# State space table products two groups behind their preparation, with three buffers, and the scan tables in the same room

## The chip, the cores and the metric

One core of one Trainium2 chip runs the whole step. The metric is the device time of one execution in microseconds (us); a repeated run of the unchanged kernel differs by 0.1%. The engines are PE (matrix products), DVE (VectorE), ACT (ScalarE), POOL (GpSimd) and SP, which here only issues transfers. Each executes its own queue strictly in order, so an instruction that waits holds up all that stand behind it on its engine.

## The reference, cut to what matters

A two-layer backbone for 256 context tokens and 2048 latent tokens of width 1024. In each layer the normalised, modulated input h goes through one wide projection; its columns feed four parallel branches (differential attention, a bidirectional diagonal state space model called S5, a gated linear recurrence, latent attention), and an output projection adds the result to the residual. The change concerns only tables that S5 derives from its weights, before any token is looked at:

```
step = exp(log_dt);  mag = exp(a_re * step)
ab   = mag * (cos(a_im * step) + i sin(a_im * step))        # per state, 16 groups x 64 states x 2 directions
f    = (ab - 1) / a;     bb = f * b                         # 16 channels per group
h[t] = ab * h[t-1] + bb u[t];     y = Re(c h) + d * u       # both directions
```

The kernel computes S5 in blocks of eight tokens. For this it needs, per group, the products of powers of ab with bb (wz) and with c (so, cp), the local 8-token kernel (psk, which becomes mp, with d on its diagonal), and per state the unit phases of 256 blocks (E). They go to DRAM as SC and ED, and the scan reads them some 1.6 ms later.

## The kernel before

`build` (L1696) runs three stages per layer: `first_stage`, `mixers`, `out_proj`. Only `first_stage` (L1607) is changed. It weaves two generators, with weights 49 and 250: `proj1` (L420) and `s5_build` (L1160).

`proj1` walks the 2304 tokens in six blocks of 384. For a block it transposes and modulates the input (`h_block`, tile pst, L299), keeps it in DRAM (HD, L440), makes five 128-wide products in the transposed layout (psF, L177 to L179, each float32 product as three of split operands), each with rotary embedding on DVE and stores to KD and QD on SP's queue (L355), and three products in token layout (psT), whose results are stored to VT (L500). These stores go on SP's queue, in the last block on POOL's.

`s5_build` first computes the powers on DVE in small operations. Then `prep(gi)` (L1270) prepares the operands of a group: wz with six and so with five operations on POOL and one on DVE (L1286), cp with six on DVE (L252 to L257), and two copies brep. The scratch tile tw has a single buffer and is used by wz, so and cp of a group in turn. `emit(gi)` (L1296) forms the products: two transposes of wz (pswz, L1302), copied by ACT into so (L1303), which SP stores to SC (L1304); four passes for psk (L1307), copied by ACT into mp (L1308). mp has one buffer for four groups: after every fourth group DVE adds Db (L1311) and SP issues eight stores (L1313). In the program emit(gi - 1) follows prep(gi). wz, so, cp and brep come from the pool sb1 with two buffers.

Then POOL doubles a base table of 16 phases (b_, with t3 as scratch, L1325), and for each pair of groups copies it into two tiles Eb (L1332) and doubles them four times up to 256 phases (L1333); SP stores them to ED (L1336). Eb0 and Eb1 have one buffer each.

What sets the order: the program's order is a priority only. A scheduler simulates the timeline of all engines and puts into each engine's queue what is ready there, the earliest in the program first (L23), so POOL's queue today mixes Eb's operations with those of prep. PE's queue alone is written by hand in the second projection. The room: sb1 and then sb are the first pools of the right side, and when the stage ends the second projection (`proj2`, L506) puts its pools there, first the tiles h of 18 KB per partition (loads at L521). A new tile waits for the old tiles whose room it takes.

Of the kernel before, what the change touches and what calls it, by code (L numbers as in the profile page):

```python
# [10 lines left out]
F32 = mybir.dt.float32  # L11
# [92 lines left out]
def run(g):  # L104
    for _ in g:
        pass


PR = (0, 0)
AVB = 2  # L110
PPB = 3
DA_A = 740
# [40 lines left out]
def pool(g, name, bufs, side="left"):  # L153
    return g.tc.tile_pool(name=name, bufs=bufs, side=side, reuse_waits="tile")
# [611 lines left out]
def diff_attn(g, l, p, p1):  # L766
# [74 lines left out]
    def pass2(pr, qb):  # L841
# [11 lines left out]
        def av_mm(batch):  # L853
            first = None
            for ki, aa, _ in batch:
                kt = kts[ki]
                for hh in range(2):
                    x = nc.tensor.matmul(av[hh * 64:(hh + 1) * 64, :n], lhsT=v[:, kt, hh * 64:(hh + 1) * 64], rhs=aa[:, hh, :n], start=(ki == 0), stop=(ki == len(kts) - 1))  # L858
                    first = first or x
            hold(g, first, batch[-1][2])  # L860

        for ki, kt in enumerate(kts):
# [11 lines left out]
            late.append((ki, aa, last))  # L874
            if len(late) > AVB:
                av_mm(late[:AVB])
                del late[:AVB]
        g.kfree = max(g.kfree, 3 * pr + 3) if qb == QLAST else g.kfree
# [9 lines left out]
def mla(g, l, p):  # L888
# [47 lines left out]
    def pass2(pr, qb):  # L936
# [17 lines left out]
        for ki, kt in enumerate(kts):  # L954
# [18 lines left out]
            late.append((ki, e, last))  # L973
            if len(late) > AVB:
                av_mm(late[:AVB])
                del late[:AVB]
        g.kfree = max(g.kfree, 3 * (pr + 2) + 3) if qb == QLAST else g.kfree
# [182 lines left out]
def s5_build(g, l, p1, pb):  # L1160
# [6 lines left out]
    def t16(nm):  # L1167
        return pb.tile([128, 16], F32, name=nm)
# [7 lines left out]
    x, mag, th = t16("x"), t16("mag"), t16("th")  # L1176
# [3 lines left out]
    k, t = t16("k"), t16("t")  # L1180
# [42 lines left out]
        renorm(nx[0], nx[1])  # L1223
        cur = nx
    yield 5
    t3 = pb.tile([128, 16, 16], F32, name="t3")
    den, fr, fi, am1 = t16("den"), t16("fr"), t16("fi"), t16("am1")
    ab = (P[0][:, 1, :], P[1][:, 1, :])
    V.tensor_tensor(den, are, are, ALU.mult)
# [24 lines left out]
    for i in range(2):  # L1254
# [5 lines left out]
        V.memset(pt[i], 0.0)  # L1260
        V.tensor_copy(pt[i][0:64, :, 7:15], pv[0:64, :, 0:8])
        V.tensor_copy(pt[i][64:128, :, 0:8][:, :, ::-1], pv[64:128, :, 0:8])
    Db = pb.tile([128, 16, 16], F32, name="Db")
    nc.sync.dma_start(Db.rearrange("p g h -> p (g h)"), g.A["s5_d"][l:l + 1, :].to_broadcast([128, 256]))
    V.tensor_tensor(Db, Db, g.id16.unsqueeze(1).to_broadcast([128, 16, 16]), ALU.mult)
    SC = g.SC[l]
# [3 lines left out]
    def prep(gi):  # L1270
        tw = pb.tile([128, 15, 16], F32, tag="tw", name="tw")
        wz = [p1.tile([128, 16, 8], F32, tag=f"wz{i}", name=f"wz{i}").rearrange("p c s -> p s c") for i in range(2)]
        pwb = [pws[i][:, gi, :].unsqueeze(2).to_broadcast([128, 8, 16]) for i in range(2)]
        bbb = [bb[i][:, gi, :].unsqueeze(1).to_broadcast([128, 8, 16]) for i in range(2)]
        cmul(E, wz[0], wz[1], pwb[0], pwb[1], bbb[0], bbb[1], tw[:, :8, :])
        so = p1.tile([128, 4, 128], F32, tag="so", name="so")
        pqb = [pq[i][:, gi, :].unsqueeze(2).to_broadcast([128, 8, 16]) for i in range(2)]
        ccb = [x_[:, gi, :].unsqueeze(1).to_broadcast([128, 8, 16]) for x_ in c_]
        car, cai = (so[:, i, :].rearrange("p (t h) -> p t h", h=16) for i in (2, 3))
        tw8 = tw[:, :8, :]  # L1280
        E.tensor_tensor(car, pqb[0], ccb[0], ALU.mult)
        E.tensor_tensor(tw8, pqb[1], ccb[1], ALU.mult)
        E.tensor_tensor(car, car, tw8, ALU.subtract)
        E.tensor_tensor(cai, pqb[0], ccb[1], ALU.mult)
        E.tensor_tensor(tw8, pqb[1], ccb[0], ALU.mult)
        V.scalar_tensor_tensor(cai, cai, -1.0, tw8, ALU.mult, ALU.subtract)  # L1286
        cp = [p1.tile([128, 15, 16], F32, tag=f"cp{i}", name=f"cp{i}") for i in range(2)]
        ptb = [pt[i][:, gi, :].unsqueeze(2).to_broadcast([128, 15, 16]) for i in range(2)]
        ccc = [c_[i][:, gi, :].unsqueeze(1).to_broadcast([128, 15, 16]) for i in range(2)]
        cmul(V if CPV else E, cp[0], cp[1], ptb[0], ptb[1], ccc[0], ccc[1], tw)  # L1290
        br_ = [p1.tile([128, 16, 8], F32, tag=f"brep{i}", name=f"brep{i}").rearrange("p c s -> p s c") for i in range(2)]
        V.tensor_copy(br_[0], bbb[0])
        V.tensor_scalar(br_[1], bbb[1], -1.0, None, ALU.mult)
        return wz, so, cp, br_

    def emit(gi, wz, so, cp, br_):  # L1296
        if gi % 4 == 0:
            g.s5mp = p1.tile([128, 4, 240], F32, tag="mp", name="mp", bufs=1)
        mp = g.s5mp
        for i in range(2):  # L1300
            ps_ = pst(g, "mm", "pswz")
            nc.tensor.transpose(ps_[:, 0:128], wz[i].rearrange("p s c -> p c s").rearrange("p c s -> p (c s)"), g.ident)  # L1302
            nc.scalar.copy(so[:, i, :], ps_[:, 0:128])  # L1303
        nc.sync.dma_start(SC[gi, :, 0:4, :], so)  # L1304
        psk = pst(g, "mm", "psk")
        for i in range(2):
            nc.tensor.matmul(psk[:, :240], lhsT=br_[i].rearrange("p s c -> p c s").rearrange("p c s -> p (c s)"), rhs=cp[i].rearrange("p t h -> p (t h)"), start=(i == 0), stop=(i == 1))  # L1307
        nc.scalar.copy(mp[:, gi % 4, :], psk[:, :240])  # L1308
        if gi % 4 == 3:
            g4 = gi - 3  # L1310
            V.tensor_tensor(mp[:, :, 112:128], mp[:, :, 112:128], Db[:, g4:g4 + 4, :], ALU.add)  # L1311
            for s in range(8):
                nc.sync.dma_start(SC[g4:g4 + 4, s:128:8, 4, :].rearrange("g p c -> p g c"), mp[s:128:8, :, (7 - s) * 16:(7 - s) * 16 + 128])  # L1313

    late = None
    for gi in range(16):
        x = prep(gi)
        yield 5
        if late:
            emit(gi - 1, *late)  # L1320
        late = x
    emit(15, *late)
    E.memset(b_[0][:, :, 0:1], 1.0)
    E.memset(b_[1][:, :, 0:1], 0.0)
    double_table(E, b_, ph, slice(0, 16), t3, 0, 4)  # L1325
    yield 5
    for g0 in range(0, 16, 2):
        gs = slice(g0, g0 + 2)
        Eb = [pb.tile([128, 2, 257], F32, tag=f"Eb{i}", name=f"Eb{i}") for i in range(2)]
        te = t3.rearrange("p (a b) c -> p a (b c)", a=2)  # L1330
        for i in range(2):
            E.tensor_copy(Eb[i][:, :, 0:16], b_[i][:, gs])  # L1332
        double_table(E, Eb, ph, gs, te, 4, 8)  # L1333
        for i in range(2):
            E.tensor_copy(Eb[i][:, :, 256], ph[8][i][:, gs])
            nc.sync.dma_start(g.ED[i, :, gs], Eb[i])  # L1336
        yield 5
# [96 lines left out]
def mixers(g, l):  # L1434
    with ExitStack() as es:
# [23 lines left out]
        with (g.tc.manual_schedule(engines={mybir.EngineType.PE}) if MAN else ExitStack()):  # L1459
            run(weave((att, 520 + 700 - DA_A), (ahead(g, ssm(), PR[1]), YW)))  # L1460

# [143 lines left out]


def first_stage(g, l):  # L1607
    with pool(g, "sb1", 2, "right") as q1, pool(g, "sb", 1, "right") as qb:
        run(weave((proj1(g, l), 49), (s5_build(g, l, q1, qb), SBW)))


# [196 lines left out]
```

## Time and profile before

| what | value |
|---|---|
| median of 3 runs | 5299.3 us (5298.6 to 5303.79) |
| profiled execution | 5296.69 us |
| its span, first to last instruction | 5294.9 us |
| PE busy | 4724.9 us (89%) |
| DVE busy | 3835.7 us (72%) |
| ACT busy | 3183.3 us (60%) |
| POOL busy | 1089.4 us (21%) |
| mean granted TensorE clock | 0.935 |

The busy shares are means over the whole span. The first stage lies at about 0 to 430 us in layer 0 and 2700 to 3080 us in layer 1; POOL is busy there for three quarters of the time, and little elsewhere. An arrow in a row of waits points to the instruction that ended the wait.

### The profile page before, as it was taken

The numbers are of one execution on the slowest core, as the hardware profiler recorded it, in microseconds if no ns is written. First come the engines' busy times: TensorE is split into PE (matmuls) and PEld (weight loads), VectorE is DVE, ScalarE is ACT, GpSimd is POOL, SyncE is SP. The second block draws the span as 40 slices with busy tenths as digits, with TensorE's granted clock in tenths as the row PEclk, the third lists the DMA queues.
The fourth block names the chain that finished last, engine by engine and source line by source line (L and its number), as shares of the span: only waits on it lengthen the run. The fifth ranks groups of instructions, "written<-read, shape, count | busy, mean of one in ns | idle before, by whom it ended". The sixth has DMA issues, their size and how long they took to land.

```text
span 5294.9 us, 81097 instructions
## 1 busy us (share of the span) xinstructions
PE 4724.9 (89%) x27920; PEld 3434.4 (65%) x27920; DVE 3835.7 (72%) x7616; ACT 3183.3 (60%) x7516; POOL 1089.4 (21%) x1323
## 2 busy tenths in 40 slices
PE   6787999999998997898987879999999989989899
PEld 5676767677665664445776757676776656654477
DVE  7655767676668886896676657676766688879877
ACT  3225878777777783235433258787777777743354
POOL 4651222222210000000227712222222100000022
PEclk8998999999998997899999989999999989989999
DMA  6555233433332124415445452334333321241253
GB/s 219 170 174 154 87 105 96 130 116 104 92 88 75 47 57 129 130 50 148 157 155 200 159 167 86 108 94 130 116 103 93 88 73 48 54 117 52 75 155 126
DMA packets 507523, 599.37 MB, mean 113 GB/s; under 512 B 147630, under 2 KB 414806, under 8 KB 507110
## 3 DMA queue, kind: packets, MB, share of 16 engines
q1 hardware_dynamic: 506630, 592.61, 37.3%
q8 instruction: 220, 3.60, 0.3%
q14 instruction: 193, 1.58, 0.1%
q0 software_dynamic: 480, 1.57, 0.1%
HBM read 378.42 MB, written 215.18 MB: 112 GB/s over the span
## 4 chain that ended last, share of the span: by engine, by line
PE 49%; DVE 18%; DMA 13%; ACT 10%; issue 4%; POOL 4%; SPq 1%; ACTq 0%; DVEq 0%; POOLq 0%
PE psav L858 5%; PE psS L870 4%; PE psF L177 4%; PE psF L178 4%; PE psF L179 4%; PE psS L817 4%; PE psmav L950 3%; ACT junk L820 3%; PE psM L961 2%; DVE nm L818 2%; DVE a L872 2%; DVE mnm L927 2%; ACT pp L871 2%; PE psM L926 2%; PE pshg L1018 2%
## 5 line engine op out<-in xcount | busy, mean ns | idle before, releaser
L818 DVE TENSOR_REDUCE nm<-psS 128x1 f32<-128x512 f32 (+1 forms) x1312 | 790.5, 626 | 351.7 <-PE psS L817 340.5
L820 ACT ACTIVATE junk<-psS,nm 128x512 bf16<-128x512 f32 (+1 forms) x1312 | 848.7, 647 | 202.2 <-DVE nm L818 182.4
L871 ACT ACTIVATE pp<-psS 128x512 f32<-128x512 f32 (+1 forms) x1184 | 654.5, 594 | 165.7 <-PE psS L870 159.6
L177 PE MATMUL psF<-h,whi 128*128 128x288 f32 x2304 | 697.9, 303 | 32.8 <-ACT whi L169 32.8
L872 DVE SCALAR_TENSOR_TENSOR a<-pp,nlam 128x512 f32<-128x512 f32 (+1 forms) x592 | 510.3, 864 | 257.6 <-ACT pp L871 256.9
L178 PE MATMUL psF<-h,whi 128*128 128x288 f32 x2304 | 687.9, 299 | 0.0
L179 PE MATMUL psF<-h,wlo 128*128 128x288 f32 x2304 | 685.1, 297 | 1.8 <-DVE wlo L173 1.8
L964 ACT ACTIVATE me<-psM 128x512 f32<-128x512 f32 (+1 forms) x592 | 345.6, 590 | 440.8 <-PE psM L963 395.1
L817 PE MATMUL psS<-ks,qs 96*128 96x512 f32 (+1 forms) x1312 | 544.5, 425 | 58.9 <-ACT junk L820 37.7
L870 PE MATMUL psS<-qs,ks 98*128 98x512 f32 (+1 forms) x1184 | 440.6, 436 | 53.9 <-ACT junk L820 38.7
L177 PEld LDWEIGHTS psF<-h,whi 128*128 128x128 f32 x2304 | 444.7, 193 | 65.3 <-ACT whi L169 34.5
L171 POOL CAST whi<-w 128x1024 fp32r<-128x1024 f32 x140 | 153.2, 1094 | 1622.0 <-PE psF L178 1299.7
L178 PEld LDWEIGHTS psF<-h,whi 128*128 128x128 f32 x2304 | 444.8, 193 | 54.8
L927 DVE TENSOR_REDUCE mnm<-psM 128x1 f32<-128x512 f32 (+1 forms) x656 | 394.1, 623 | 70.9 <-PE psM L926 69.0
L179 PEld LDWEIGHTS psF<-h,wlo 128*128 128x128 f32 x2304 | 441.5, 192 | 3.1 <-DVE wlo L173 3.1
L817 PEld LDWEIGHTS psS<-ks,qs 96*128 96x128 f32 x1312 | 255.2, 197 | 165.5 <-ACT junk L820 98.4
L870 PEld LDWEIGHTS psS<-qs,ks 98*128 98x128 f32 x1184 | 203.3, 192 | 236.3 <-ACT junk L820 136.4
L173 POOL TENSOR_TENSOR wlo<-w,whi 128x1024 fp32r<-128x1024 f32 x140 | 350.3, 2502 | 11.2
L967 DVE TENSOR_TENSOR macc<-macc,me 128x1024 f32<-128x1024 f32 x256 | 311.2, 1216 | 45.0 <-ACT me L964 44.2
L950 PE MATMUL psmav<-me,mv 128*64 128x512 f32 (+1 forms) x1184 | 318.0, 631 | 13.7 <-ACT me L964 7.9
L858 PE MATMUL psav<-a,dav 128*64 128x512 f32 (+1 forms) x1184 | 309.5, 643 | 18.2 <-DVE a L872 18.2
L961 PE MATMUL psM<-qs,ks 98*128 98x512 f32 (+1 forms) x592 | 269.8, 456 | 49.2 <-ACT me L964 21.6
(451 smaller groups left out, 10191.2 us busy)
## 6 DMA issues: line engine op xcount, KB each, us to landing
w<-wF SPq DMA_DIRECT2D x152, 512.0 KB
h<-HD SPq DMA_DIRECT2D x64, 576.0 KB
wmod<-w_mod SPq DMA_DIRECT2D x48, 512.0 KB
HD<-hhi SPq DMA_DIRECT2D x12, 1536.0 KB
HD<-hlo SPq DMA_DIRECT2D x12, 1536.0 KB
GX<-ev SPq DMA_DIRECT2D x128, 144.0 KB
gt<-GX SPq DMA_DIRECT2D x36, 512.0 KB
PF<-ev SPq DMA_DIRECT2D x96, 144.0 KB
```

The lines of the kernel that those rows point to most:

```text
L177: nc.tensor.matmul(out, lhsT=w_hi, rhs=x_hi, start=start, stop=False)
L178: nc.tensor.matmul(out, lhsT=w_hi, rhs=x_lo, start=False, stop=False)
L179: nc.tensor.matmul(out, lhsT=w_lo, rhs=x_hi, start=False, stop=stop)
L817: nc.tensor.matmul(ps[:, :kn], lhsT=qs[0:96, i, t * 128:(t + 1) * 128], rhs=key_cols(ks[i], k0, kn)[0:96], start=True, stop=True)
L818: nc.vector.tensor_reduce(nm[:, i, t, ci:ci + 1], ps[:, :kn], axis=AX.X, op=ALU.max, negate=True)
L820: nc.scalar.activation(out=junk[:, :kn], in_=ps[:, :kn], func=AF.Exp, bias=nm[:, i, t, ci:ci + 1], accum_out=sm[:, i, t, ci:ci + 1])
L858: x = nc.tensor.matmul(av[hh * 64:(hh + 1) * 64, :n], lhsT=v[:, kt, hh * 64:(hh + 1) * 64], rhs=aa[:, hh, :n], start=(ki == 0), stop=(ki = ...
L870: nc.tensor.matmul(ps[:, :n], lhsT=key_cols(ks[2 * hh + m], kt * 128, 128), rhs=qs[:, 2 * hh + m, :n], start=True, stop=True)
L871: nc.scalar.activation(out=pp[:, m, :n], in_=ps[:, :n], func=AF.Exp)
L872: last = nc.vector.scalar_tensor_tensor(aa[:, hh, :n], pp[:, 1, :n], nlam, pp[:, 0, :n], ALU.mult, ALU.add)
L927: nc.vector.tensor_reduce(nm[:, i, t, ci:ci + 1], ps[:, :kn], axis=AX.X, op=ALU.max, negate=True)
L950: x = nc.tensor.matmul(av[i * 64:(i + 1) * 64, :n], lhsT=v[:, kts[ki], i * 64:(i + 1) * 64], rhs=e[:, i, :n], start=(ki == 0), stop=(ki == ...
```

## The change

A constant S5LAG = 2 is added. The loop over groups keeps the prepared operands in a list and emits the oldest when more than two are there, with a further yield of 0.1 behind each emission; the last two are emitted behind the loop, with yields of 2. The pool sb1 has three buffers. The tile t3 (scratch of bb and, later, of the doublings) and the tile Db share one buffer under one tag; for the doublings t3 is taken anew. The tiles Eb0 and Eb1 leave the pool sb and take turns in the three buffers of so in sb1.

```diff
--- before.py
+++ after.py
@@ -107,6 +107,7 @@
 
 
 PR = (0, 0)
+S5LAG = 2
 AVB = 2
 PPB = 3
 DA_A = 740
@@ -1223,7 +1224,7 @@
         renorm(nx[0], nx[1])
         cur = nx
     yield 5
-    t3 = pb.tile([128, 16, 16], F32, name="t3")
+    t3 = pb.tile([128, 16, 16], F32, tag="t3", name="t3")
     den, fr, fi, am1 = t16("den"), t16("fr"), t16("fi"), t16("am1")
     ab = (P[0][:, 1, :], P[1][:, 1, :])
     V.tensor_tensor(den, are, are, ALU.mult)
@@ -1260,7 +1261,7 @@
         V.memset(pt[i], 0.0)
         V.tensor_copy(pt[i][0:64, :, 7:15], pv[0:64, :, 0:8])
         V.tensor_copy(pt[i][64:128, :, 0:8][:, :, ::-1], pv[64:128, :, 0:8])
-    Db = pb.tile([128, 16, 16], F32, name="Db")
+    Db = pb.tile([128, 16, 16], F32, tag="t3", name="Db")
     nc.sync.dma_start(Db.rearrange("p g h -> p (g h)"), g.A["s5_d"][l:l + 1, :].to_broadcast([128, 256]))
     V.tensor_tensor(Db, Db, g.id16.unsqueeze(1).to_broadcast([128, 16, 16]), ALU.mult)
     SC = g.SC[l]
@@ -1312,21 +1313,25 @@
             for s in range(8):
                 nc.sync.dma_start(SC[g4:g4 + 4, s:128:8, 4, :].rearrange("g p c -> p g c"), mp[s:128:8, :, (7 - s) * 16:(7 - s) * 16 + 128])
 
-    late = None
+    late = []
     for gi in range(16):
-        x = prep(gi)
+        late.append((gi, prep(gi)))
         yield 5
-        if late:
-            emit(gi - 1, *late)
-        late = x
-    emit(15, *late)
+        if len(late) > S5LAG:
+            k, x = late.pop(0)
+            emit(k, *x)
+            yield 0.1
+    for k, x in late:
+        emit(k, *x)
+        yield 2
+    t3 = pb.tile([128, 16, 16], F32, tag="t3", name="t3")
     E.memset(b_[0][:, :, 0:1], 1.0)
     E.memset(b_[1][:, :, 0:1], 0.0)
     double_table(E, b_, ph, slice(0, 16), t3, 0, 4)
     yield 5
     for g0 in range(0, 16, 2):
         gs = slice(g0, g0 + 2)
-        Eb = [pb.tile([128, 2, 257], F32, tag=f"Eb{i}", name=f"Eb{i}") for i in range(2)]
+        Eb = [p1.tile([128, 2, 257], F32, tag="so", name=f"Eb{i}") for i in range(2)]
         te = t3.rearrange("p (a b) c -> p a (b c)", a=2)
         for i in range(2):
             E.tensor_copy(Eb[i][:, :, 0:16], b_[i][:, gs])
@@ -1605,7 +1610,7 @@
 
 
 def first_stage(g, l):
-    with pool(g, "sb1", 2, "right") as q1, pool(g, "sb", 1, "right") as qb:
+    with pool(g, "sb1", S5LAG + 1, "right") as q1, pool(g, "sb", 1, "right") as qb:
         run(weave((proj1(g, l), 49), (s5_build(g, l, q1, qb), SBW)))
```

## Rows read from the trace of the kernel before

**Rows 1.** Windows view, stretch; length, busy us (count) of PE, PEld, DVE, ACT, POOL; clock; DMA
```profile
105.00:345.00 240.00, 190.61 (x925) 166.38 (x926) 152.20 (x331) 64.25 (x146) 180.47 (x398) 0.90 0.48 159
2790.00:3025.00 235.00, 193.76 (x991) 169.66 (x992) 159.64 (x349) 68.18 (x157) 188.59 (x409) 0.93 0.52 175
```

**Rows 2.** Waits of PE, layer 0, 105 to 345 us: us in total, times, longest
```profile
PE pswz L1302 <- POOL wz L257: 18.0, 6, 7.5
PE pswz L1302 <- ACT mp L1308: 11.8, 3, 6.2
PE psk L1307 <- DVE cp L254: 5.3, 2, 4.3
PE pswz L1302 <- POOL wz L254: 4.5, 5, 1.8
...
PE psk L1307 <- DVE cp L257: 2.1, 3, 0.9
PE psF L177 <- ACT x L372: 1.6, 1, 1.6
```

**Rows 3.** Waits of PE, layer 1, 2790 to 3025 us
```profile
PE psk L1307 <- DVE cp L254: 11.2, 5, 4.7
PE pswz L1302 <- POOL wz L257: 9.2, 4, 5.5
PE psk L1307 <- DVE cp L257: 5.8, 4, 4.8
PE pswz L1302 <- POOL wz L254: 5.8, 4, 2.3
PE pswz L1302 <- ACT mp L1308: 4.5, 2, 3.4
```

**Rows 4.** Timeline of POOL, layer 1: start us, us, operation, idle before
```profile
2791.71 1.43 POOL L252 TENSOR_TENSOR wz<-pws,bb 128x128 f32<-128x128 f32 x2 [0.88 <-DVE bb L254]
...
2847.51 0.40 POOL L253 TENSOR_TENSOR tw<-pws,bb 128x128 f32<-128x128 f32 x1
...
2856.28 0.40 POOL L1285 TENSOR_TENSOR tw<-pq,c 128x128 f32<-128x128 f32 x1
...
2860.52 0.65 POOL L253 TENSOR_TENSOR tw<-pws,bb 128x128 f32<-128x128 f32 x1 [0.34 <-DVE cp L257]
```

**Rows 5.** Timeline of DVE, layer 1, the same group
```profile
2856.72 0.47 DVE L1286 SCALAR_TENSOR_TENSOR so<-so,tw 128x128 f32<-128x128 f32 x1 [2.84 <-POOL tw L1285]
...
2859.63 0.81 DVE L257 TENSOR_TENSOR cp<-cp,tw 128x240 f32<-128x240 f32 x1
```

**Rows 6.** POOL by line, 2780 to 3045 us: busy us, mean ns, idle before, releasers
```profile
L254 POOL TENSOR_TENSOR Eb<-Eb,t 128x32 f32<-128x32 f32 (+3 forms) x32 | 16.5, 517 | 1.1
...
L254 POOL TENSOR_TENSOR wz<-wz,tw 128x128 f32<-128x128 f32 x16 | 10.6, 664 | 0.2
...
L1284 POOL TENSOR_TENSOR so<-pq,c 128x128 f32<-128x128 f32 x14 | 6.9, 490 | 0.0
L1332 POOL COPY Eb<-b 128x32 f32<-128x32 f32 x16 | 5.5, 342 | 20.4 <-DMA ED<-Eb 20.4
...
L257 POOL TENSOR_TENSOR b<-b,t 128x16 f32<-128x16 f32 (+3 forms) x4 | 2.5, 634 | 0.0
```

**Rows 7.** Timeline of SP's queue, layer 1
```profile
3038.99 1.00 SPq L1336 DMA_DIRECT2D ED<-Eb  x2
...
3042.09 3.07 SPq L521 DMA_DIRECT2D h<-HD  x4
```

**Rows 8.** Timeline of SP's queue, layer 0
```profile
368.28 3.90 SPq L521 DMA_DIRECT2D h<-HD  x2
```

**Rows 9.** Timeline of PE, layer 1, first matmul on h
```profile
3109.55 0.61 PE L177 MATMUL psF<-h,whi 128*128 128x288 f32 x1 [8.25 <-ACT whi L169]
```

**Rows 10.** Timeline of PE, layer 0, first matmul on h
```profile
480.77 0.61 PE L177 MATMUL psF<-h,whi 128*128 128x288 f32 x1 [8.55 <-ACT whi L169]
```

**Rows 11.** Timeline of POOL, layer 1, end of the stage
```profile
3069.49 0.61 POOL L500 DMA_DIRECT2D VT<-evT  x1 [34.61 <-ACT evT L499]
```

## The prediction

> **What bounds the kernel now.** The page gives a PE-bound kernel, but the change touches only the first stage of each layer, where the first projection (proj1) runs woven with the building of the state space (S5) tables. So I read that stage, not the whole. First the view by stretches: between the first and the last table product PE works 190.6 of 240 us in layer 0 and 193.8 of 235 us in layer 1, so it idles 49 and 41 us, and no other engine is busier [rows 1]. Then the waits of PE in these two stretches. Nearly all of the idle time stands ahead of S5's own instructions: 41.7 us in the five rows shown of layer 0 and 36.5 us in the five of layer 1, against 1.6 us ahead of proj1's matmuls [rows 2, 3]. PE executes in order, so a table transpose (pswz) whose operand isn't there holds up proj1's matmuls behind it. The waits are of three kinds: for POOL's wz 18.0 + 4.5 + 9.2 + 5.8 = 37.5 us, for DVE's cp 5.3 + 2.1 + 11.2 + 5.8 = 24.4 us, and for ACT's copy into mp, which itself waits for a buffer, 11.8 + 4.5 = 16.3 us. Sum 78.2 us.
>
> Then why the operands are late. Follow one group on POOL and DVE: its first use of tw starts at 2847.51, its last POOL use (L1285) at 2856.28, DVE carries on at 2856.72 and starts the last cp at 2859.63, and only then can POOL begin the next group's tw, at 2860.52 [rows 4, 5]. tw has one buffer, so this ring of 13.0 us is the pace of preparation; the two buffers of wz, so, cp and brep seldom are. Of the ring 2856.68 - 2847.51 = 9.2 us is POOL's. A group's preparation has eleven kinds of operation there, from L254 with 10.6 us to L1284 with 6.9 us for all 16 groups, 92.2 us together; the seven of them that stand in the ring take 3.75 us a group by their means. The rest of the 9.2 us are operations on Eb and on other groups that lie between them in POOL's queue [rows 6].
>
> **The change part by part.** (a) The lag of two. emit(k) now follows prep(k+2) in program order, where it followed prep(k+1). Order in the program is only a priority here: the queues are written in the order in which operations become ready in the scheduler's simulated time. S5 starts late (the first wz of layer 1 at 2791.71, 16 groups at 13 us to go) [rows 4], while the weave gives it about one group for each of proj1's blocks; so its products are the oldest work whenever they are ready, with either lag. I therefore give the lag itself nothing; its upper bound is all 78.2 us, its lower bound 0, since an emission that is moved down adds no instruction and can at worst be as late as its operand already is.
>
> (b) Three buffers instead of two for wz, so, cp, brep. No work is added, and no wait of PE shown is for a buffer of these [rows 2, 3]; I give it nothing (bounds 0 and 13 us, a ring once a layer). mp and tw keep their single buffer, so the 16.3 us for mp stay.
>
> (c) Eb moves into the so buffers and is thereby behind all 16 so tiles in POOL's queue; and t3, Db and the new t3 share one buffer, so the doubling of the base table (its temporary is that t3) waits for the last Db addition, behind emit(15). Today Eb's work lies among the preparation. This is the part that I expect to act. Without it POOL's part of the ring falls from 9.2 to 3.75 us, DVE's stays at 2859.63 + 0.81 - 2856.72 = 3.7 (I take 4.0) with about 1 us of handing over, so the ring falls from 13.0 to 8.7 us. PE's waits for wz and cp both hang on this ring (cp waits for DVE, and DVE for POOL's tw). Foreign work was 5.4 of 9.2 us, 59%; I take that share of the waits to go: 0.59 x (37.5 + 24.4) = 36.5 us over both layers. The bounds are 0 (all returns, as PE's order is made tighter by the same amount) and 61.9.
>
> (d) What is late next. Preparation takes 16 x 8.7 = 139 us from 2791.7, to 2931; the last emits with their Db addition take some 15 us (a ring and a copy), to 2946; then the base table, 11.5 us (six kinds of operation on b, 2.5 us the largest); then the Eb operations with 103.9 us (eight kinds, the largest 16.5 us) and their waits for the ED stores, 20.4 us now [rows 6] (bounds 0 to 40, since three buffers serve two tiles of a group). Eb ends at 2946 + 11.5 + 124 = 3081 where it ended at 3035, 46 us later. Behind it: the ED store and then, in SP's queue, the loads of h for the second projection, which are to lie in the room of these tiles; today ED goes at 3039 and h at 3042 in layer 1, h at 368 in layer 0 [rows 7, 8]. The first matmul on h starts at 3109.55 and 480.77 [rows 9, 10]. With today's distance of 3 to 7 us from Eb's end, h is issued at 3088; its four issues take 3.1 us, and with 5 us of flight, my estimate, it has landed at 3096, under a start that 18 us of gain would put at 3091: 5 us lost. In layer 0 the h loads move to 414, 66 us ahead of their use. But SP executes in order: where h is queued in front of proj1's last stores (KD, QD) and Eb is later than was planned, these stores, their buffers and proj1's last block stand. POOL has the same knot, with the stores of VT at 3069.49 behind Eb [rows 11]. For both together I take 7 us, over both layers; 0 is the lower bound and 46 us in each layer the upper. The Db load now waits for bb's cmul; its first use, behind the fourth group, is four rings later and hides it.
>
> The sum: -36.5 + 5 + 7 = -24.5 us. The profiled execution took 5296.7 us (span 5294.9), so 5272.2; the median of the runs is 2.6 us above that execution, so 5274.8 us, rounded to 5275.
>
> **One rule against it.** Operations of one shape differ on POOL: 128x128 takes 490 ns in the mean at L1284 and 664 at L254 [rows 6]. The Trainium skill (SBUF — State Buffer, "Who interferes with whom") says that a VectorE instruction with two SBUF inputs and a GpSimd instruction that reads SBUF exclude each other for a whole instruction. The rows show the spread, not its cause; taken strictly the rule does not hold here, as DVE (159.6) and POOL (188.6) are busy 348 us in 235 [rows 1], which can only be if many of their instructions run beside each other. By the rule a closer ring would buy little; the third rival below works that out from rows.
>
> **The rivals.** First, the change doesn't do what it says: PE's queue is drawn up for the faster ring, and PE is as early for each operand as before, 78.2/32 = 2.4 us a group. Then the 78.2 us stay and so does the time, 5299 give or take 10, if the tail hides. For it: the stalls are differences between planned and real time, and the plan moves with the change. Against it: waits for ED, which nobody planned so long, no longer stand ahead of wz.
>
> Second, PE loses all S5 stalls, those for mp too, as POOL runs ahead and three buffers take up the jitter: -78.2 with a tail of 12 is -66, 5233. Against it: mp is still single, and its eight stores per four groups come closer together.
>
> Third, on the other side: POOL and DVE don't speed up, and the Eb tail decides. If POOL's preparation (92.2 us) and DVE's work (159.6/235 x 139 = 94 us) can hardly run together, preparation takes 186 us, a ring of 11.6. Then the gain is a third, about -12, and Eb ends at 2791.7 + 186 + 15 + 11.5 + 124 = 3128, h lands at 3143 with ED's store, and the first matmul on h slips from 3109.55 by 34 us; the stores behind h in layer 0 take 5 more. That is +27, 5326. It decides as soon as the last ED store of layer 1 is issued after some 3095. The skill's rule above is this rival's mechanism. For it: the ED waits and the single tw buffer are unchanged; against it: the overlap in rows 1.
>
> **How the numbers follow.** Forecast 0.40 (own range 5255 to 5288), nothing gained 0.22 (5289 to 5310), all stalls gone 0.16, the tail decides 0.22. What differs from no change by less than 0.2%, 10.6 us, can't be told from it. Faster are the forecast and the second: 0.56; same 0.22; slower 0.22. The range reaches from the second rival, 5236, to near the third, 5320; half of each lies outside, 2 in 10 together. The rest of the kernel is scheduled by the same simulation, and shifted starts may reorder some of it by several us either way; that is inside these widths.
>
> **What would show it.** Right: no Eb between the tw steps on POOL, a ring near 9 us, PE's waits for wz and cp down by half or more, Eb in one block at the end, ED's last store some 46 us later in layer 1. (a) is wrong if pswz is moved past proj1's matmuls so that its waits vanish with the ring still at 13 us. (d) is wrong if SP shows long waits at the h loads or POOL holds the VT stores. The forecast is wrong if PE's S5 waits stay near 78 us, or if the second projection starts later than its stage ends by more than now.

## The result: 1% slower, and the profile after

The changed kernel takes 5349.98 us (median of 5 runs, 5342.91 to 5351.73) against 5299.06 for the kernel before (5285.18 to 5303.79): ratio 1.0101, 95% interval 1.0084 to 1.0119. The forecast of 5275 us, and its sign, were wrong. The third rival, "the tail decides" (5326 us), came nearest.

The profiled execution of the changed kernel has a span of 5349.2 us, 54 more than before. Where they arise can be read from five marks in each trace: the first product psF of proj1, its last psT, the first matmul on h of the second projection, and POOL's first and last operation on wz and on Eb.

| us from the span's start | before | after |
|---|---|---|
| layer 0: last psT | 433.1 | 438.7 |
| layer 0: first matmul on h | 464.5 | 484.3 |
| layer 1: first psF | 2704 | 2721 |
| layer 1: wz on POOL | 2792 to 3010 | 2809 to 2984 |
| layer 1: Eb on POOL | 2814 to 3034 | 3000 to 3148 |
| layer 1: last ED store issued | 3040 | 3149 |
| layer 1: last psT | 3079.2 | 3084.9 |
| layer 1: first matmul on h | 3109.5 | 3164.4 |

The stage itself, from first psF to last psT, became 11 us shorter in layer 1 (375.2 to 364.1) and 7 us longer in layer 0 (409.2 to 415.9). The gap between it and the second projection grew from 31.4 to 45.6 us in layer 0 and from 30.3 to 79.5 us in layer 1: 63 us together. That is the whole loss and more. Behind the gaps little changed: from the first matmul on h of layer 1 to the last result both kernels take 2180 us, and from that of layer 0 to the first psF of layer 1 the changed kernel takes 3 us less. Nor does the granted clock explain it: its mean is 0.88 and 0.91 of full speed in the two stages, and 0.94 and 0.95 behind the gaps, in both kernels.

What answers to [rows 1] is this, from the windows view: layer 0 in the same stretch, layer 1 from the first wz to the first Eb, and the block of Eb.

```profile
105.00:345.00 240.00, 192.60 (x940) 170.61 (x941) 131.51 (x334) 65.32 (x150) 119.76 (x263) 0.89 0.46 149
2809.00:3000.00 191.00, 162.84 (x846) 144.22 (x845) 125.59 (x315) 61.14 (x142) 105.02 (x208) 0.92 0.49 169
3000.00:3150.00 150.00, 91.66 (x385) 72.78 (x383) 45.77 (x89) 34.69 (x84) 87.90 (x225) 0.75 0.58 170
```

POOL's busy time in layer 0 fell from 180 to 120 us, as Eb left this stretch, and yet PE's rose only from 190.6 to 192.6. In the third row POOL does 88 us of Eb while PE works 92 of 150 us. PE's waits in layer 0, 105 to 345 us, beside [rows 2]:

```profile
PE pswz L1303 <- POOL wz L258: 15.3, 6, 4.1
PE pswz L1303 <- ACT so L1304: 11.2, 3, 5.5
PE pst L300 <- DVE dg L288: 9.2, 3, 4.8
PE pswz L1303 <- ACT mp L1309: 5.7, 3, 2.8
PE pst L300 <- ACT t L305: 3.3, 1, 3.3
```

The waits for cp are nearly gone in layer 0; a wait of pswz behind ACT's copies of so (3.4 us before) and waits of proj1's own transposes stand in their place. Ahead of all table products (pswz and psk) PE waited 49.2 + 41.0 us in the stretches 95 to 450 and 2780 to 3100 us before, and 35.2 + 28.0 after: 27 us less, of which the length of the two stages shows 5. Ahead of proj1's own products PE waited 19 us more in the same stretches (23.9 + 11.0 before, 39.8 + 14.6 after).

Now the tail. SP's queue in layer 1, before (the second four loads of h, which [rows 7] don't have) and after (start us, us, operation):

```profile
3096.25 2.46 SPq L521 DMA_DIRECT2D h<-HD  x4
```

```profile
3112.46 2.52 SPq L522 DMA_DIRECT2D h<-HD  x4
...
3129.56 20.04 SPq L1341 DMA_DIRECT2D ED<-Eb  x4
3151.41 2.33 SPq L522 DMA_DIRECT2D h<-HD  x4
3153.78 18.21 SPq L533 DMA_DIRECT2D w<-wF  x3
```

The last four ED issues hold the queue for 20 us, in most of which SP waits for POOL to finish Eb (16.2 us at one of them). The second four loads of h follow, and the weights w follow them. PE's waits from 3084 to 3165 us, and its first matmul on h, beside [rows 9]:

```profile
PE psF L178 <- ACT whi L170: 47.4, 1, 47.4
PE psS L818 <- DMA ks<-KD: 13.2, 1, 13.2
```

```profile
3164.43 0.61 PE L178 MATMUL psF<-h,whi 128*128 128x288 f32 x1 [47.42 <-ACT whi L170]
```

Before, the first of the two waits was 8.25 us [rows 9], and the second was this:

```profile
PE psS L817 <- DMA ks<-KD: 3.4, 1, 3.4
```

The releaser named, ACT's split of w, is only the last link. The chain that ended last goes back through w, h and ED to POOL's last Eb, and from there to an earlier ED store (start us, us, what; 3080 to 3175 us, excerpt):

```profile
3129.56 9.49 DMA ED<-Eb
...
3148.53 0.73 POOL Eb L258
3149.28 2.04 DMA ED<-Eb
3151.83 0.50 SPq L522
...
3153.78 9.54 DMA w<-wF
3163.34 1.05 ACT whi L170
```

[Rows 10] had been misread: that row isn't the first matmul on h of layer 0, which came at 464.5 us.

POOL by line from 2790 to 3160 us shows why the block is so long; beside [rows 6] (busy us, mean ns, idle time before):

```profile
L255 POOL TENSOR_TENSOR Eb<-Eb,t 128x32 f32<-128x32 f32 (+3 forms) x32 | 15.1, 471 | 2.3
...
L1282 POOL TENSOR_TENSOR so<-pq,c 128x128 f32<-128x128 f32 x13 | 10.7, 822 | 24.3 <-DMA SC<-so 24.1 <-ACT evT L500 0.2
L258 POOL TENSOR_TENSOR wz<-wz,tw 128x128 f32<-128x128 f32 x16 | 9.9, 619 | 1.2
...
L254 POOL TENSOR_TENSOR tw<-pws,bb 128x128 f32<-128x128 f32 x16 | 8.0, 497 | 32.8 <-DVE cp L258 30.9 <-DVE rsv L190 1.8
...
L1337 POOL COPY Eb<-b 128x32 f32<-128x32 f32 x16 | 4.6, 293 | 54.7 <-DMA ED<-Eb 54.7
```

The Eb operations themselves are a little quicker than before, but POOL now waits 54.7 us for ED stores to land before it may reuse a buffer (20.4 before). And the ring is not free either: POOL waits 24.1 us for the stores of so, in spite of three buffers, and 30.9 us for DVE's last use of tw. These two waits before, 2780 to 3045 us:

```profile
POOL tw L253 <- DVE cp L257: 9.9, 6, 3.2
POOL so L1281 <- DMA SC<-so: 5.6, 1, 5.6
```

### The profile page after: what moved, and what is told of

It reads as the page before. It is cut to its first block, busy times and chain, and to the rows that moved or that the text cites. A ratio compares the mean times of both kernels' runs of the same rounds, so it can differ in the third digit from the quotient of the medians.

```text
span 5349.2 us, 81141 instructions
## 1 busy us (share of the span) xinstructions
PE 4732.8 (88%) x27920; PEld 3450.5 (65%) x27920; DVE 3805.8 (71%) x7616; ACT 3177.9 (59%) x7516; POOL 1079.5 (20%) x1323
## 4 chain that ended last, share of the span: by engine, by line
PE 51%; DVE 18%; DMA 12%; ACT 10%; issue 4%; POOL 3%; SPq 2%; ACTq 0%; DVEq 0%; POOLq 0%
PE psav L859 5%; PE psS L871 4%; PE psF L178 4%; PE psF L179 4%; PE psF L180 4%; PE psS L818 4%; PE psmav L951 3%; ACT junk L821 3%; PE psM L962 2%; DVE nm L819 2%; DVE a L873 2%; ACT pp L872 2%; PE psM L927 2%; DVE mnm L928 2%; PE psop L178 2%
## 5 line engine op out<-in xcount | busy, mean ns | idle before, releaser
L927 PE MATMUL psM<-ks,qs 96*128 96x512 f32 (+1 forms) x656 | 263.7, 438 | 55.0 <-DMA ks<-KRD 26.7
```

## The experiments

Times are medians; a ratio is to the kernel before, run beside it on the same chip. The places of marks are from one profiled execution each. "Last ED" below is the issue of the last ED store of layer 1, "gap" the time from the last psT to the first matmul on h.

**Lag one, rooms shared.** The changed kernel with

```diff
-S5LAG = 2
+S5LAG = 1
```

> The changed kernel with a lag of one group, and so two buffers, the rest as changed: Eb in the room of so, one buffer for t3 and Db. Theory (the tail: all of Eb's doubling now stands behind the last product, and what follows the stage waits for it): the tail is kept, so about 5345 us, 5325 to 5365. Rival (the lag: a later emission keeps the buffers longer and delays the stage): back to about 5300 us, 5285 to 5315.

Measured: 5356.33 us, ratio 1.0112 [1.0077, 1.0147]; last ED 3172, gap 82 us. The loss needs neither the lag of two nor the third buffer. What the two together are worth isn't resolved: the interval is some 18 us wide to either side and holds the changed kernel's.

**One Eb pair doubled.** The changed kernel, in which only the first pair of Eb is built, and stored for all eight:

```diff
-        Eb = [p1.tile(...) for i in range(2)]
+        if g0 == 0:
+            Eb = [p1.tile(...) for i in range(2)]
...
-        double_table(E, Eb, ph, gs, te, 4, 8)
+        if g0 == 0:
+            double_table(E, Eb, ph, gs, te, 4, 8)
```

> The changed kernel with Eb doubled for the first pair of groups alone and stored eight times (it leaves out seven of eight doublings in each layer, so ED holds the phases of the first pair everywhere). Theory (the tail): the gap between the last projection product and the first product on h falls from 46 and 80 us to the 32 and 31 us of before or less, 5350 - 63 = 5287 us, 5265 to 5300. Rival (the lag): over 5325 us, since all products are emitted as late as in the changed kernel.

Measured: 5284.9 us, ratio 0.9978 [0.9965, 0.9992]; Eb ends at 2997, gaps 30.2 and 30.1 us as before the change. Without the tail the change gains 11 us. PE's waits ahead of table products are 36.6 + 31.2 us here, near those of the changed kernel. So this is about all that the shorter ring is worth: 0.2%, not 0.7%. SP's queue and PE in layer 1:

```profile
2999.14 14.14 SPq L1345 DMA_DIRECT2D ED<-Eb  x15
...
3086.84 3.28 SPq L522 DMA_DIRECT2D h<-HD  x4
```

```profile
3100.17 0.61 PE L178 MATMUL psF<-h,whi 128*128 128x288 f32 x1 [7.12 <-ACT whi L170]
```

**Only t3 and Db share.** The kernel before with

```diff
-    t3 = pb.tile([128, 16, 16], F32, name="t3")
+    t3 = pb.tile([128, 16, 16], F32, tag="t3", name="t3")
...
-    Db = pb.tile([128, 16, 16], F32, name="Db")
+    Db = pb.tile([128, 16, 16], F32, tag="t3", name="Db")
...
+    t3 = pb.tile([128, 16, 16], F32, tag="t3", name="t3")
     E.memset(b_[0][:, :, 0:1], 1.0)
```

> The kernel before with one thing of the change: t3, Db and the t3 of the doublings share one buffer; lag one, two buffers, Eb in its own two tiles. Theory A (this shared buffer is what puts the whole doubling behind the last addition of Db): the tail appears, Eb's first operation after the last product, 5325 to 5350 us. Theory B (the room of so does it): no effect, 5290 to 5308 us.

Measured: 5380.26 us, ratio 1.0159 [1.014, 1.0179]; Eb from 3004 to 3161, gaps 60.5 and 91.1 us. One kilobyte of shared scratch alone makes the tail, and a longer one than the whole change:

```profile
3147.96 14.08 SPq L1337 DMA_DIRECT2D ED<-Eb  x4
...
3163.90 2.23 SPq L521 DMA_DIRECT2D h<-HD  x4
```

**Only Eb in so's buffers.** The kernel before with

```diff
-        Eb = [pb.tile([128, 2, 257], F32, tag=f"Eb{i}", name=f"Eb{i}") for i in range(2)]
+        Eb = [p1.tile([128, 2, 257], F32, tag="so", name=f"Eb{i}") for i in range(2)]
```

> The kernel before with one edit: the Eb tiles are taken from the two so buffers; t3 and Db keep rooms of their own, the lag stays one. Theory (the tail decides, and either sharing alone is enough for it): Eb can't start before the last so tiles are given back, near 3000 us in layer 1, so it becomes one block of some 150 us behind the products, its last store goes out near 3150, the first matmul on h slips by 40 to 60 us in layer 1 and 10 to 30 in layer 0, and the time is 5335 to 5375 us. Rival (only the buffer shared by t3 and Db keeps Eb back; with the base table doubled early, Eb slips in between the so tiles): Eb still starts before 2900 us in layer 1, time 5290 to 5310 us.

Measured: 5328.92 us, ratio 1.006 [1.0039, 1.0081]; Eb from 2984 to 3148, gaps 39.5 and 67.2 us.

```profile
3129.75 19.86 SPq L1336 DMA_DIRECT2D ED<-Eb  x4
...
3152.02 2.41 SPq L521 DMA_DIRECT2D h<-HD  x4
```

The place is as the theory had it, the time 6 us below its range. From first psF to first matmul on h the two layers lose 55 us against the kernel before, nearly as much as with the whole change (59); the rest of the kernel took 26 us less, which no run explains. Either sharing alone puts Eb behind the products. With both and the same lag it was 5356: the two don't add up, as both make the same block.

**The block's gate.** The changed kernel with the scratch of the doublings in tw's buffer (to make room for the longer tw, the small tile den takes the tile k; the three later runs with scratch in tw's buffer have this too):

```diff
-        tw = pb.tile([128, 15, 16], F32, tag="tw", name="tw")
+        tw = pb.tile([128, 16, 16], F32, tag="tw", name="tw")[:, :15, :]
...
-    t3 = pb.tile([128, 16, 16], F32, tag="t3", name="t3")
+    t3 = pb.tile([128, 16, 16], F32, tag="tw", name="t3")
     E.memset(b_[0][:, :, 0:1], 1.0)
```

> The changed kernel with the doubling's scratch taken from the buffer of tw instead of the one that t3 and Db share, so that the base table waits for POOL's own last tw only and no longer for the last Db addition behind the last products. Theory (the gate at the Db addition is a small part of the tail; the block of about 149 us of Eb is the large one): Eb starts 10 to 16 us earlier than 3000 us in layer 1, and the time is 5333 to 5345 us. Rival (Eb waits for the so buffers in any case, whose last stores go out behind the last products): Eb starts at 3000 us as before, time 5345 to 5355 us.

Measured: 5348.83 us, ratio 1.0098 [1.0076, 1.012]. From POOL's last wz to its first Eb it is 12 us (3009 to 3021) where it was 16. Layer 1 began 22 us later than in the changed kernel; counted from its first psF, Eb starts after 278 us, and there after 279. The theory fell, and the time is the rival's: taking the gate at Db away gains nothing that can be seen. That so's buffers are what holds Eb instead is argued, not shown.

**Half of Eb on DVE.** The same kernel, with

```diff
+        Q = V if g0 % 4 else E
+        te = (tv if g0 % 4 else t3).rearrange("p (a b) c -> p a (b c)", a=2)
...
-        double_table(E, Eb, ph, gs, te, 4, 8)
+        double_table(Q, Eb, ph, gs, te, 4, 8)
```

> The kernel of the run with the scratch in tw's buffer, in which every second pair of groups has its Eb doubled on DVE with a scratch of its own, the others on POOL as before. Theory (the length of the Eb block sets the start of the second projection): POOL has half of the operations, the block falls from 149 to 80 to 100 us, the last ED store goes out at 3080 to 3100 us in layer 1, the first matmul on h comes 40 to 50 us earlier than at 3164 us, and the time is 5285 to 5310 us. Rival (three buffers and their ED stores set the pace of the block, or DVE's share of it stands in front of the splits that PE waits for): the block stays over 120 us or PE's waits for DVE grow by as much as the tail falls, time 5325 to 5350 us.

Measured: 5346.28 us, ratio 1.0092 [1.0064, 1.0119]; last ED 3129, first matmul on h 3151.3. The theory fell, the rival held (block 130 us): with half of its work gone POOL waits nearly as long for ED as before, and DVE waits too. Waits of POOL, 2990 to 3130 us, and of DVE, 2990 to 3110 us:

```profile
POOL Eb L1339 <- DMA ED<-Eb: 48.2, 5, 24.1
```

```profile
DVE Eb L1339 <- DMA ED<-Eb: 34.1, 6, 10.1
```

The pace of the block is set by the three buffers and the issue and landing of their stores more than by the operations.

**ED stored by POOL's queue.** The changed kernel with

```diff
-            nc.sync.dma_start(g.ED[i, :, gs], Eb[i])
+            nc.gpsimd.dma_start(g.ED[i, :, gs], Eb[i])
```

> The changed kernel with the 16 stores of ED in each layer issued by POOL instead of SP. Theory (SP is held: its last four ED issues stand 20 us in the queue, and the loads of h and of the weights for the second projection stand behind them): the loads go out 20 to 30 us earlier, the first matmul on h of layer 1 comes at 3115 to 3140 instead of 3164 us, and the time is 5305 to 5330 us. Rival (room: the second four loads of h are to lie in the buffers that Eb holds, so they wait for the last ED store to land, whoever issues it): they still go out at about 3150 us, the first matmul on h stays within 10 us of 3164, time 5340 to 5355 us.

Measured: 5322.17 us, ratio 1.005 [1.0034, 1.0065]; last ED 3127, first matmul on h 3141.5. The time fits the theory, the mechanism is the rival's. First POOL's wait for ED, 2780 to 3180 us, then SP's wait at the loads of h, 3060 to 3190 us:

```profile
POOL Eb L1337 <- DMA ED<-Eb: 25.3, 9, 5.0
```

```profile
SPq L522 <- DMA ED<-Eb: 18.5, 2, 16.9
```

```profile
3099.30 2.25 SPq L522 DMA_DIRECT2D h<-HD  x4
3129.95 2.45 SPq L522 DMA_DIRECT2D h<-HD  x4
```

SP is no longer held by ED's issues, and still the second four loads of h wait until the last ED store has landed, because they are to lie in Eb's room. In layer 1 the block is 17 us shorter (131.5 for 148.5), as POOL waited 25 instead of 55 us for its buffers to come free, and the first matmul on h comes 16 us sooner after the first psF; in layer 0 it is 2 us. The rest of the 28 us isn't seen in the profiled execution, which was the slowest of its seven (5332.68).

**Both remedies at once.** The kernel with half of Eb on DVE, with the store of the run before it:

```diff
-            nc.sync.dma_start(g.ED[i, :, gs], Eb[i])
+            nc.gpsimd.dma_start(g.ED[i, :, gs], Eb[i])
```

> The kernel of the run with half of the Eb pairs on DVE, with ED stored by POOL's queue as well. Each of the two alone brought the last ED store of layer 1 from 3149 to 3127 to 3129 us. Theory (the start of the second projection follows the landing of the last ED store, as its buffers are the room of h): the block shrinks again, the last ED store goes out at 3100 to 3115 us, the first matmul on h of layer 1 comes at 3115 to 3135 us, time 5300 to 5325 us. Rival (with the block shorter, the order of the second projection's loads in SP's queue holds it): the first matmul on h stays at 3140 us or later, time 5325 to 5350 us.

Measured: 5316.36 us, ratio 1.0033 [1.002, 1.0047]; last ED 3112, h at 3119.86, first matmul 3133.0. The theory held.

**Half of the pairs left out.** The changed kernel, in which only every second pair of Eb is built, and stored for two:

```diff
-        Eb = [p1.tile(...) for i in range(2)]
+        if g0 % 4 == 0:
+            Eb = [p1.tile(...) for i in range(2)]
...
-        double_table(E, Eb, ph, gs, te, 4, 8)
+        if g0 % 4 == 0:
+            double_table(E, Eb, ph, gs, te, 4, 8)
```

> The changed kernel with the doubling of four of the eight pairs of Eb left out in each layer; every pair that is doubled is stored for two pairs, so all 16 stores remain. It stands between the changed kernel (eight pairs, 5350 us) and the run with one pair (5285 us). Theory (the tail costs nothing until the last ED store of layer 1 goes out after some 3095 us, and then one for one): the block ends near 3075 us, the first matmul on h comes at 3100 to 3110 us, time 5280 to 5300 us. Rival (POOL's work behind the products costs in proportion, by a busy port or a busy queue): half of the 65 us between the two kernels remains, 5310 to 5325 us.

Measured: 5301.72 us, ratio 1.0006 [0.9994, 1.0018]: nearer the theory, but just out of its range; the rival fell. Its profiled execution was the slowest of its 12 (5320.55), so it is read above all for the order of things. PE's wait and SP's queue in layer 1:

```profile
PE psS L818 <- DMA ks<-KD: 15.0, 1, 15.0
```

```profile
3068.36 2.20 SPq L1345 DMA_DIRECT2D ED<-Eb  x2
3077.42 2.39 SPq L522 DMA_DIRECT2D h<-HD  x4
3080.61 0.53 SPq L806 DMA_DIRECT2D qs<-QD  x1
3081.24 0.97 SPq L792 DMA_DIRECT2D ks<-KD  x1
3082.99 9.81 SPq L792 DMA_DIRECT2D ks<-KD  x7
```

The first loads of h, at 3042 before, now come between ED and the loads of ks, on which PE starts the attention's products: 15.0 us of wait where the kernel before has 3.4. So there are two knots. ED, h and ks in one in-order queue cost some 10 us as soon as ED runs into proj1's end (a gap of 41.2 us against 30.3; that ks is what makes it longer is read from the order, no run moves ks alone). The room of h costs nearly one for one when ED ends later still: from the interleaved kernel below to the one in which t3 and Db share, the distance from last psT to last ED grows by 65 us and the gap by 54.

**Interleaved by hand.** The changed kernel's rooms with a lag of one, the base table ahead of the first group, and

```diff
+        if gi % 2:
+            eb_pair(gi - 1)
+            yield 5
```

behind each second group, where eb_pair builds and stores one pair, its scratch in tw's buffer.

> The changed kernel with its shared rooms kept (Eb in the so buffers, three buffers, t3 and Db in one), but with another program order: the base table is doubled ahead of the first group, one pair of Eb tiles is built after every second group's preparation, with its scratch in the buffer of tw, and products follow one group behind. Theory (what costs the time is that the Eb work comes as one block behind the products; the shared rooms by themselves cost little): Eb starts before 2870 us in layer 1 and its last store goes out near 3040 to 3060, the first matmul on h comes at 3100 to 3125 us, and the time is 5290 to 5315 us. Rival (sharing the so buffers is itself dear, since every pair of Eb takes two of three buffers from the products and their stores): the ring grows beyond 14 us a group, PE's waits ahead of the table products exceed the 90 us of the kernel before over both layers, time 5325 to 5370 us.

Measured: 5351.94 us, ratio 1.0098 [1.0082, 1.0115]. The theory fell. Eb starts at 2830 us, but wz now runs from 2809 to 3092, 18 us a group, and the last ED is at 3110 all the same. PE's waits, layer 0 and layer 1:

```profile
PE pswz L1306 <- POOL wz L255: 35.9, 8, 7.7
PE psk L1311 <- DVE cp L255: 13.4, 4, 9.5
```

```profile
PE pswz L1306 <- POOL wz L255: 29.1, 6, 7.1
PE pswz L1306 <- POOL wz L258: 12.2, 6, 5.8
```

The rival held in its place: the ring is beyond 14 us, and PE's waits ahead of table products are 58.4 + 48.3 us (49.2 + 41.0 before). But of the 58 us that this profiled execution is longer than that before, the two stages and gaps hold only 24; 32 lie behind layer 1's first matmul on h, where no run says why. So Eb among the products holds up the ring and behind them makes a tail, and what the first costs in time is shown for less than half of the loss.

**Two edits to the kernel before.** A scratch tile of its own for POOL's part of the ring:

```diff
+        tp = pb.tile([128, 8, 16], F32, tag="tp", name="tp")
-        cmul(E, wz[0], wz[1], pwb[0], pwb[1], bbb[0], bbb[1], tw[:, :8, :])
+        cmul(E, wz[0], wz[1], pwb[0], pwb[1], bbb[0], bbb[1], tp)
...
-        tw8 = tw[:, :8, :]
+        tw8 = tp
```

> The kernel before with a scratch tile of POOL's own for wz and so, while DVE's cp keeps tw, so that POOL can prepare the next group while DVE still works on cp. Theory (the ring over the single tw sets the pace of preparation, and PE's stalls hang on it): ring from 13 us to 10 to 11, PE's waits at S5's instructions down by 20 to 40 us over both layers, 5265 to 5285 us. Rival (POOL is full of work anyway: 215 of 250 us): 5293 to 5306 us, PE's waits as before.

Measured: 5324.92 us, ratio 1.0056 [1.0037, 1.0075]: both missed. The ring did fall, from 13.6 to 11.6 us (185 us of wz by 16 groups), and PE's waits ahead of table products from 90 to 76 us, without any gain in time. POOL's busy time before was 195 of 250 us (2780 to 3030), not 215. The stage became 18 us longer in layer 1, with these waits of PE from 3000 to 3090 us, the first of them 8.4 us before:

```profile
PE pso L338 <- ACT x L364: 16.8, 1, 16.8
PE pso L338 <- ACT x L372: 8.9, 1, 8.9
```

They are proj1's own. What in the new queues puts them there was not tested. And ED from POOL's queue in the kernel before:

```diff
-            nc.sync.dma_start(g.ED[i, :, gs], Eb[i])
+            nc.gpsimd.dma_start(g.ED[i, :, gs], Eb[i])
```

> The kernel before with one edit: its ED stores are issued by POOL's queue instead of SP's. In the changed kernel the same edit cut POOL's waits for ED from 54.7 to 25.3 us in layer 1. Theory (in the kernel before POOL waits 20 us for ED among the preparation, which lengthens the ring): those waits halve, PE's waits ahead of the table products fall by 5 to 15 us, time 5284 to 5296 us. Rival (the waits are hidden or return elsewhere): 5296 to 5306 us, or slower if POOL pays for each issue in its own queue.

Measured: 5310.89 us, ratio 1.0021 [1.001, 1.0032]. POOL's wait for ED fell as expected, but its 16 issues are work in its queue, and the wait for DVE's cp doubled (9.9 us before), while PE's waits ahead of table products rose from 90 to 99.5 us. POOL, 2780 to 3065 us:

```profile
L1336 POOL DMA_DIRECT2D ED<-Eb x16 | 9.5, 595 | 0.6 <-POOL Eb L257 0.6
L1332 POOL COPY Eb<-b 128x32 f32<-128x32 f32 x16 | 6.1, 381 | 3.8 <-DMA ED<-Eb 3.8
```

```profile
POOL tw L253 <- DVE cp L257: 20.8, 6, 7.8
```

What POOL saved at one wait it paid elsewhere; the theory fell, and a measure that helps the block didn't help the ring.

**All kernels in one table.** The first three columns are layer 1, us from the start. "Stages and gaps" is the time from first psF to first matmul on h, both layers together, less that of the kernel before.

| kernel | last ED | second loads of h | first matmul on h | stages and gaps | median |
|---|---|---|---|---|---|
| one pair doubled | 3013 | 3086.8 | 3100.2 | -10 | 5284.9 |
| before | 3040 | 3096.3 | 3109.5 | 0 | 5299.1 |
| own scratch | 3045 | 3101.2 | 3115.7 | +14 | 5324.9 |
| before, POOL's queue | 3061 | 3107.0 | 3120.1 | +9 | 5310.9 |
| half of the pairs | 3069 | 3103.7 | 3118.4 | +7 | 5301.7 |
| interleaved | 3110 | 3117.8 | 3136.0 | +24 | 5351.9 |
| DVE and POOL's queue | 3112 | 3119.9 | 3133.0 | +28 | 5316.4 |
| POOL's queue | 3127 | 3130.0 | 3141.5 | +41 | 5322.2 |
| half on DVE | 3129 | 3138.5 | 3151.3 | +52 | 5346.3 |
| Eb in so's buffers | 3149 | 3152.0 | 3156.5 | +55 | 5328.9 |
| after | 3149 | 3151.4 | 3164.4 | +59 | 5350.0 |
| scratch in tw | 3162 | 3170.5 | 3183.4 | +48 | 5348.8 |
| t3 and Db share | 3162 | 3163.9 | 3176.7 | +86 | 5380.3 |
| lag one | 3172 | 3174.5 | 3178.7 | +70 | 5356.3 |

Up to 3069 the last ED store precedes the second loads of h by 34 us or more and doesn't set them. From 3110 on they follow it within 2 to 10 us, and the first matmul follows them by 4 to 18. The medians follow less strictly. What the stages and gaps leave of a profiled execution's difference lies in the rest of the kernel, and goes from 26 us less (Eb in so's buffers) to 34 us more (interleaved); no run explains it. A median can also lie up to 19 us from the profiled execution. No version tried beats the kernel before and computes everything; even with half of Eb left out the changed kernel only draws level. A lag of two with Eb in its old room wasn't tried: by the sizes of the tiles the third buffers take 5.9 KB more per partition, of which the two shared rooms give 5.0 back.

## Why the prediction was wrong, step by step

**(a) the lag: right.** It was given nothing, and nothing is seen: 5350 with two, 5356 with one, within the intervals. The run with one also has two buffers, so two effects that cancel aren't excluded.

**(b) three buffers: not shown wrong.** With lag one and two buffers POOL waits 32.5 us for so's stores in layer 1, with three 24.1. But that the so buffers seldom bind [rows 2, 3] no longer held: that wait was 5.6 us before. It stands ahead of Eb, and is 38.9 us where only t3 and Db share, with Eb in its own room; so it comes with the quicker ring and not with Eb in so's buffers.

**(c) the ring: half right.** No Eb lies between the tw steps, as predicted. But the ring fell from 13.6 us (218 us of wz by 16 groups) to 10.9 (175 by 16), not from 13.0 to 8.7. The sum took POOL's part without Eb plus DVE's part; the trace shows new waits between them, for so's stores and longer ones for cp. It also counted seven of a group's eleven steps on POOL, those on tw; three more stand among them in the program, 1.6 us a group by their means. PE's waits ahead of the products fell by 27 us, not 36.5, and of these the stages got back 5 in the changed kernel and, in the run without the tail, 8.5: most of the rest, 19 us in the changed kernel, reappeared ahead of proj1's own products. The whole gain, 11 us, was mis-sized by a factor of three. With 11 us in place of 36.5 the sum would have come out at no change.

**(d) the tail: the step that failed.** It was priced at 5 + 7 = 12 us and cost 63. Its mechanism was named (the ED store, the room of h, SP's order), its size was not. Eb's end was put at 3081 and came at 3148. Of the 67 us, 17 are the later start of layer 1's stage (layer 0's gap is 14 us longer and its stage 7, less 3 in what lies between, and 1 us of an earlier start); 36 the slower preparation (175 for 139); 24 the block (148.5 for 124), whose ED waits were 54.7 us, above the upper bound of 40; the way from the last wz to the first Eb was 10 shorter. The working already had the first matmul wait 5 us for h, so nothing was left to hide what came on top: it turned into time nearly one for one. It also let the path end where h has landed, with a flight of 5 us that no row gives. In the trace the path goes on through w, queued behind h: 9.5 us for w and 1 for its split, and the matmul starts 13 us after the issue of h, where the working had 8. And it trusted that layer 0 had 66 us in hand (50, by its true first matmul on h). It lost 14 there: ED's last store came at 448, not 414, in front of the loads of ks, for which PE waited 15.1 us (5.6 before).

**The rivals.** "Doesn't do what it says" fell: PE's waits did fall. "All stalls gone" fell. "The tail decides" was right in its place and nearly in its sizes: a ring of 11.6 (10.9), Eb's end at 3128 (3148), a slip of 34 us (55), decisive from a last ED of 3095, where the table has its turn between 3069 and 3110. It got 0.22. Its reason was another, though. The rule from the Trainium skill (SBUF — State Buffer, "Who interferes with whom") would make POOL's operations slow beside DVE's; the same steps took 488 ns at so's subtraction before and 494 after, 664 and 611 at wz, and all eleven of the preparation together 92.2 and 91.6 us. The ring is long by its waits for buffers and stores, not by slower operations. That the rule "does not hold here" was more than [rows 1] can bear, as they add up all of DVE's instructions. A single pair bears it better: DVE's step on so at 2856.72 [rows 5] and a product on POOL (start 2856.64, 0.46 us), both with two inputs in SBUF, overlap by 0.4 us, as far as the rough spans on POOL go. How far the port costs POOL anything here no run isolates.

Two signs in the profile before could have told: the first projection had 49 + 41 us of PE idle, but a faster ring frees only those waits that nothing else takes up; and [rows 7] put ED's last store 56 us ahead of the second loads of h (3096.25), so a move of 46 us with a block that waits for its own stores had hardly any room for error.

## What to carry to other kernels

When side work shares a room with the work that it used to lie between, ask first where the scheduler can still put it: a shared buffer can be an ordering, and a kilobyte of it cost 1.6% here. Price the side work at the length it has alone, with the waits of its own stores, and set its new end against the first load that will lie in its room. A stall ahead of one engine's instructions is an upper bound of the gain, and a loose one: of 90 us of stalls 27 went and 11 us were gained. A run without the side work shows about how much moving it can gain.

## What was not expected of the hardware

Moving the same stores from SP's queue to POOL's let their buffers go sooner: POOL's waits for ED in the block fell from 54.7 to 25.3 us. No run separates SP's order from the transfer, but the longest of those waits, 14.6 us, can be taken apart: the tile was done at 3123.1, SP issued its store at 3129.6, behind other loads, and it landed 9.5 us later. From POOL's queue a store landed 6.4 us after its issue in the median. In the kernel before with that edit each issue takes POOL 595 ns in the mean. The six arithmetic steps of Eb take POOL 456 to 517 ns in the mean among the preparation and 395 to 471 in the block, where DVE is busy 46 of 150 us; in the run with half of Eb on DVE they take DVE 278 to 295 ns.
